# Query projection as two units of seven block products, w_down chunks moved around the last P7, idle TensorE instructions in two feed-forward jobs

## The chip, the core and the metric

The kernel runs on one core of a Trainium2 chip. A core has a matrix engine (TensorE, PE in the profile, with its weight loads as PEld), VectorE (DVE), ScalarE (ACT), GpSimd (POOL) and SyncE (SP). Each engine works off its own queue of instructions in a fixed order and waits for others by semaphores. DMAs are issued from SP's queue (plain copies) and, where the transfer adds to its destination, from POOL's. The metric is the device time of one execution in microseconds; lower is better.

## What is computed

One encoder layer on 512 tokens of width 1024, all in float32. After two mixers come memory cross-attention and a gated feed-forward layer; the change concerns these two.

```python
def memory_cross_attention(hn, memn, w_q, w_k, w_v, w_o):
    q = (hn @ w_q).reshape(bsz, seq, XATTN_HEADS, XATTN_HEAD_DIM)
    k = (memn @ w_k).reshape(bsz, MEM_LEN, XATTN_HEADS, XATTN_HEAD_DIM)
    v = (memn @ w_v).reshape(bsz, MEM_LEN, XATTN_HEADS, XATTN_HEAD_DIM)
    s = jnp.einsum('blhd,bmhd->bhlm', q, k) * (XATTN_HEAD_DIM ** -0.5)
    p = jax.nn.softmax(s, axis=-1)
    o = jnp.einsum('bhlm,bmhd->blhd', p, v).reshape(bsz, seq, D_MODEL)
    return o @ w_o

def swiglu(hn, w_gate, w_up, w_down):
    return (jax.nn.silu(hn @ w_gate) * (hn @ w_up)) @ w_down
...
    h = h + memory_cross_attention(rms_norm(h, xattn_norm_g[i]), memn, ...)
    h = h + swiglu(rms_norm(h, ffn_norm_g[i]), w_gate[i], w_up[i], w_down[i])
```

There are 4 heads of 256, 256 memory rows, and a feed-forward width of 2816.

## The kernel before

**Precision.** Every float32 operand is split into a high part (ACT, a cast to fp32r, L85) and a low part (DVE, the difference, L86). A matrix product is then three fp32r matmuls: high by high, high by low, low by high (`mm3`).

**Weights and their plan.** All weight blocks, each 128 x 1024 elements (512 KB), stand in one list, `plan`, in the order in which TensorE uses them. `next_w` takes the next entry. At that point it also issues what has come due for later entries: a plain load from SP up to three entries ahead (`LOADS`; three `raw` buffers), the split into high and low two entries ahead (`SPLITS`), and other transfers by the distance written beside them. `begin` runs these. The tile framework's scheduler, which goes by a simulated timeline, then decides the order of the instructions on each engine, except that instructions marked by `keep_in_program_order` (here `in_order`) keep their order among themselves.

**Block products.** The ten units of the feed-forward layer (512 columns each of w_gate and w_up, L1408 on) use Strassen's scheme in Winograd's form: the 2 x 2 blocks of tokens and weights are multiplied in seven block products P1 to P7 instead of eight, each 24 matmuls of 256 columns (`product`, L1306 on). Sums of weight blocks are made in part by adding DMAs of POOL onto tile `t` (`onto`, L177) and on DVE (L180); sums of activations on DVE. A job runs P5, P6, (P1 of the next unit), P7, (P2 of the next unit), P4, P3. P6, P7 and P4 add up in one PSUM bank `px`; after P6 and after P7 ACT copies the bank's state (`u2` L1421, `u3` L1428). In the last job two chunks of w_down's first product stand between P6 and P7, and nothing between P7 and P4. w_down is done in the same scheme over the tokens' 256-row halves; its weight sums are made by DMA alone, ahead of time, in DRAM scratch `dsum`: for each of 24 pieces a plain copy from SP (`start`, L236) and, three plan entries later, an adding DMA from POOL (`add`, L239), from entry 14 on every third entry.

**Queries.** hn is turned to feature-major form by TensorE transposes (`to_feat`, L485) and split. Each head is one `feat` over two blocks of w_q: 96 matmuls of 256 columns for the first head (two token parts) and 48 of 512 for each other head. Then come `scores` (24 matmuls of 256 columns, softmax on DVE and ACT), `turn_probs` (8 transposes) and `values` (12 matmuls of 512 columns), the values of a head after the scores of the next. w_k and w_v go before, in blocks of half length (256 memory rows); w_xo goes after.

Of the kernel before, what the change touches and what calls it, by code (L numbers as in the profile page):

```python
# [30 lines left out]
XH = 4  # L31
# [21 lines left out]
def hybrid_layer_kernel(  # L53
# [108 lines left out]
    def plan_unit(w, c0):  # L162

        kh = KD // 2
        b = lambda i, j: block(w, i * kh, kh, c0 + 256 * j, 256)
        r = {}

        def fresh(nm):
            r[nm] = (wp if nm == "b11" else stp[0]).tile([P, kh, 256], F32, tag="raw" if nm == "b11" else nm,
                                                         name=nm, bufs=3 if nm == "b11" else 2)  # L170
            return r[nm]

        def plain(nm, src):
            return lambda: nc.sync.dma_start(fresh(nm), src)

        def onto(nm, src):
            return lambda: nc.gpsimd.dma_start(r[nm], src, accum_op=ALU.add)  # L177

        def tt(o, x, y, op):
            nc.vector.tensor_tensor(r[o], r[x], r[y], op)  # L180
# [9 lines left out]
        return {q: ((w, c0, q), loads, made) for q, loads, made in (  # L190
            (1, [(4, plain("b11", b(0, 0)))], make("b11")),
            (2, [(4, plain("b21", b(1, 0)))], make("b21")),
            (5, [(7, plain("t", b(0, 0))), (5, onto("t", b(0, 1))), (5, plain("b22", b(1, 1)))],
             make("t", "t", "t", "b22", ALU.add)),
            (6, [], lambda: (make("t", "b11", "t", "b11", ALU.subtract)(), tt("t", "t", "b21", ALU.add))[0]),
            (7, [], make("b11")),
            (4, [], make("t")),
            (3, [], make("b22")))}

    def plan_units(units, down):  # L200


        made = [plan_unit(*u) for u in units]
# [25 lines left out]
    def plan_sums(first, step):  # L229


        more = {5: lambda c: down_block(0, 1, c), 7: lambda c: down_block(1, 1, c),
                6: lambda c: down_sum(5, c), 4: lambda c: down_sum(6, c)}

        def start(q, i, jc, c):
            tc.keep_in_program_order(nc.sync.dma_start(down_sum(q, c), down_block(i, jc, c)))  # L236

        def add(q, c):
            nc.gpsimd.dma_start(down_sum(q, c), more[q](c), accum_op=ALU.add)  # L239

        j = first
        for q, i, jc in ((5, 0, 0), (7, 0, 1), (6, 1, 1), (4, 1, 0)):
            for c in range(CHUNKS):
                plan[j][1].append((0, lambda x=(q, i, jc, c): start(*x)))
                plan[j + step][1].append((0, lambda x=(q, c): add(*x)))
                j += step
# [39 lines left out]
    for c0 in range(0, D, 256):  # L286
        plan_feat(w_q, c0, KD)
# [8 lines left out]
    plan_sums(first_copy + 2, 3)  # L296
# [71 lines left out]
    def tokm(w, c0, act, nk, evac, ntok=NT, last=2, kpt=2, hook=None, cut=None, t0=0):  # L368
# [6 lines left out]
        for wi in range(nw):  # L375
            hi, lo = next_w(w, wi * kpt, kpt, c0, 512)
            held.append((wi, hi, lo))
            if hook is not None and wi == nw - last:
                hook()
# [99 lines left out]
    def to_feat(src, hi, lo, tsl, full=None, part=(0, 1)):  # L479

        for q in part:
            ps = aux("ptr", (P, 4, P))
            for j in range(4):
                k = 4 * q + j
                nc.tensor.transpose(ps[:, j, :], src[:, k * P:(k + 1) * P], ident)  # L485
            split(hi[:, 4 * q:4 * q + 4, tsl], lo[:, 4 * q:4 * q + 4, tsl], ps)
            if full is not None:
                nc.scalar.copy(full[:, 4 * q:4 * q + 4, tsl], ps)
# [3 lines left out]
    def norm_feat(src, g, hi, lo, tsl, ss=None, full=None):  # L492
        xs = xsp[0].tile([P, D], F32, tag="xs", name="xs", bufs=2)
        rms_scale(src, g, xs, ss)
        later(0.6, lambda: to_feat(xs, hi, lo, tsl, full))
# [602 lines left out]
    hn_hi, hn_lo = token_slot("hn")  # L1098
    hn = (hn_hi, hn_lo)
# [16 lines left out]
    for t in range(NM):  # L1116
        later(0.2 + t, lambda t=t: mem_norm(t))

# [15 lines left out]
    def feat_norm(g, hi, lo, full=None):  # L1134
        return lambda t, ss: norm_feat(h[:, t, :], g, hi, lo, slice(t * P, (t + 1) * P), ss, full)

    mg = (mg_hi, mg_lo)
    for half in range(2):
        tokm(w_out, half * 512, mg, KD, add_evac(half, 0, feat_norm(g_x, hn_hi, hn_lo)))
# [3 lines left out]
    shift = ap_.tile([P, APART[0]], F32, name="shift")  # L1143
    nc.gpsimd.memset(shift, 0.0)
    kt_hi = ap_.tile([P, KD, M], F32R, name="kt_hi")
    kt_lo = ap_.tile([P, KD, M], F32R, name="kt_lo")
    vt_hi = ap_.tile([P, NM, D], F32R, name="vt_hi")
    vt_lo = ap_.tile([P, NM, D], F32R, name="vt_lo")
# [4 lines left out]
    def v_evac(half):  # L1153
        def f(t, ps):
            cs = slice(half * 512, half * 512 + 512)
            split(vt_hi[:, t, cs], vt_lo[:, t, cs], ps)
        return f

    for c0 in range(0, D, 256):
# [5 lines left out]
    ot_hi = slot("D", (P, KD, T), F32R, "ot_hi")  # L1165
    ot_lo = slot("E", (P, KD, T), F32R, "ot_lo")
    qs = {}

    def q_evac(m, j, ps):
        if j == 0:  # L1170
            qq = mq_tile("qq", 0).rearrange("p (h k t) -> p h k t", h=2, k=2)
            qs[m // 2] = (qq[:, 0], qq[:, 1])
        q_hi, q_lo = qs[m // 2]
        split(q_hi[:, j, :], q_lo[:, j, :], ps)

    def scores(hd):
        q_hi, q_lo = qs.pop(hd)
        scale = XD ** -0.5
        probs = []
        for i in range(2):  # L1180
# [7 lines left out]
            prob = ap_.tile([P, 2, M], F32, tag="prob", name="prob", bufs=2)  # L1188
            probs.append(prob)
# [3 lines left out]
            for tt in range(2):  # L1193
                nc.scalar.activation(prob[:, tt, :], ps[:, tt, :], AF.Exp, bias=nm[:, tt:tt + 1],
                                     scale=scale, accum_out=sm[:, tt:tt + 1])
            nc.vector.reciprocal(rs, sm)
            for tt in range(2):
                nc.vector.tensor_scalar(prob[:, tt, :], prob[:, tt, :], rs[:, tt:tt + 1], None, ALU.mult)
        return probs

    def turn_probs(hd, probs):
        p_hi = ap_.tile([P, NM, T], F32R, tag="p_hi", name="p_hi", bufs=2)
        p_lo = ap_.tile([P, NM, T], F32R, tag="p_lo", name="p_lo", bufs=2)
        for mt in range(NM):
            ps = aux("ppt", (P, NT, P))
            for t in range(NT):
                nc.tensor.transpose(ps[:, t, :], probs[t // 2][:, t % 2, mt * P:(mt + 1) * P], ident)
# [3 lines left out]
    def values(hd, p_hi, p_lo):  # L1211
        for dt_ in range(2):
            ps = bank("po")
            cs = slice(hd * XD + dt_ * P, hd * XD + dt_ * P + P)
            for mt in range(NM):
                mm3(ps, (vt_hi[:, mt, cs], vt_lo[:, mt, cs]), (p_hi[:, mt, :], p_lo[:, mt, :]), mt == 0, mt == NM - 1)
            split(ot_hi[:, 2 * hd + dt_, :], ot_lo[:, 2 * hd + dt_, :], ps)

    pts = []
# [13 lines left out]
    tokm(w_xo, 0, ot, KD, add_evac(0, 1, None), hook=lambda: values(XH - 1, *pts.pop()))  # L1233
# [49 lines left out]
    K0, K1, T0, T1 = slice(0, 4), slice(4, 8), slice(0, 256), slice(256, 512)  # L1283
# [22 lines left out]
    def product(ps, u, q, start):  # L1306

        hi, lo = next_w(u[0], u[1], q)
        for j in range(2):
            cs = slice(j * P, (j + 1) * P)  # L1310
            for k in range(4):
                a = (hi[:, k, cs], lo[:, k, cs])
                b = (ops[q][0][:, k, :], ops[q][1][:, k, :])
                for i, (x, y) in enumerate(((0, 0), (0, 1), (1, 0))):
                    nc.tensor.matmul(ps[:, j, :], a[x], b[y], start=start and j == k == i == 0,  # L1315
                                     stop=k == 3 and i == 2, skip_group_check=True)
        tick(2.7)

    def unit_bank(name):
        return bank(name).rearrange("p (j t) -> p j t", j=2)  # L1320

    def unit_start(u):
        x, v = unit_bank("px"), unit_bank("pv")
        product(x, u, 1, True)
# [10 lines left out]
    def unit_second(u, v):  # L1335
        product(v, u, 2, False)
# [70 lines left out]

    for i, u in enumerate(UNITS):  # L1408
# [3 lines left out]
        product(q, u, 5, True)  # L1412
# [5 lines left out]
        product(x, u, 6, False)  # L1418
# [12 lines left out]
        if not final:  # L1431
            unit_second(UNITS[i + 1], begun[1])
        V.tensor_tensor(u3, q, u3, ALU.subtract)
        put(u, 1, T1, u3)
        product(x, u, 4, False)
# [4 lines left out]
        product(q, u, 3, False)  # L1440
# [133 lines left out]
```

## Time and profile before

| | us |
|---|---|
| runs shown (3): median, lowest, highest | 913.34, 913.03, 913.4 |
| profiled execution, device time | 914.3 |
| its span from first to last instruction | 912.5 |
| busy in it: PE, DVE, ACT, POOL | 899.1, 607.5, 460.1, 93.6 |

The page of the profile gives each engine's busy time; the stretches show it part by part; the chain of waits follows what ended last back through the engines; the groups list instructions by source line, engine and tile with their mean duration; a timeline lists them one by one. A matmul's listed duration includes the length of the engine's pipeline, so that durations of matmuls overlap; what a matmul costs in a row of them is the distance of their starts. DMA rows give size and time from issue to landing.

### The profile page before, as it was taken

Reading aid. Unit: us, or ns where it says so; the run is one execution under the profiler, and the core shown is the slowest. Engines: PE = TensorE matmul, PEld = TensorE weight load, DVE = VectorE, ACT = ScalarE, POOL = GpSimd, SP = SyncE. Lnnn points to the kernel's source line nnn. Section 1 sums busy time; section 2 is a strip of 40 time slices with the busy share of each in tenths; the row PEclk is TensorE's granted clock in tenths of the full one; section 3 lists DMA queues with packets and bytes.
Section 4 is the critical chain, followed back from the end, with each engine's and each line's share of the span. In section 5 each row is a group of like instructions: output and inputs, shape, how many; then the busy total and the mean of one; then the engine's idle time right before and its main releaser. Section 6 shows DMA issues by size and latency. Waiting matters only on the chain.

```text
span 912.5 us, 14202 instructions
## 1 busy us (share of the span) xinstructions
PE 899.1 (99%) x5546; PEld 789.3 (86%) x5546; DVE 607.5 (67%) x1002; ACT 460.1 (50%) x674; POOL 93.6 (10%) x157
## 2 busy tenths in 40 slices
PE   9999999999999999999999999999999999999996
PEld 6788888888888887889898888899999999888875
DVE  5596662888753235758545444787778777889875
ACT  5542985244374334346434433655454554655663
POOL 1004220000025300002000001000000000000010
PEclk9999999999999999999999999999999999999998
DMA  7445273675546656776995317416455553246672
GB/s 242 137 125 145 71 180 120 183 201 136 141 135 157 146 173 184 237 227 194 258 279 136 82 64 236 110 43 158 125 146 148 124 155 101 70 138 198 196 231 101
DMA packets 105158, 142.25 MB, mean 156 GB/s; under 512 B 13170, under 2 KB 73090, under 8 KB 105091
## 3 DMA queue, kind: packets, MB, share of 16 engines
q1 hardware_dynamic: 90114, 119.88, 41.0%
q0 software_dynamic: 12384, 20.42, 13.2%
q10 hardware_dynamic: 2592, 1.05, 0.5%
q8 instruction: 43, 0.70, 0.3%
q14 instruction: 25, 0.20, 0.1%
HBM read 134.54 MB, written 29.85 MB: 180 GB/s over the span
## 4 chain that ended last, share of the span: by engine, by line
PE 90%; ACT 4%; DMA 2%; DVE 1%; issue 1%; POOL 0%; POOLq 0%; SPq 0%; DVEq 0%; ACTq 0%
PE pf L327 33%; PE pt L327 14%; PE px L1315 12%; PE dx L327 6%; PE pq L1315 6%; PE dq L327 3%; PE pv L1315 3%; PE dv L327 2%; PE pk L764 2%; DMA wraw<-in_w_up_dram 1%; PE ptr L485 1%; PE po L327 1%; PE psc L327 1%; ACT whi L85 1%; PE psv L1012 1%
## 5 line engine op out<-in xcount | busy, mean ns | idle before, releaser
L86 DVE TENSOR_TENSOR wlo<-wraw,whi 128x1024 fp32r<-128x1024 f32 (+1 forms) x133 | 157.7, 1186 | 131.7 <-ACT whi L85 130.1
L85 ACT CAST whi<-wraw 128x1024 fp32r<-128x1024 f32 (+1 forms) x133 | 135.9, 1022 | 180.0 <-PE pf L327 83.4
L327 PE MATMUL pf<-xn,whi 128*128 128x512 f32 x448 | 140.0, 392 | 0.0
L327 PEld LDWEIGHTS pf<-xn,whi 128*128 128x128 f32 x448 | 83.5, 188 | 17.1 <-issue 0.2
L327 PE MATMUL pf<-xn,wlo 128*128 128x512 f32 x224 | 87.5, 391 | 0.0
L1315 PE MATMUL px<-fn,whi 128*128 128x256 f32 x480 | 83.8, 277 | 1.5 <-ACT u L1428 1.5
L1315 PEld LDWEIGHTS px<-fn,whi 128*128 128x128 f32 x480 | 72.6, 188 | 1.8 <-ACT u L1428 1.7
L85 ACT CAST whi<-b 128x1024 fp32r<-128x1024 f32 x40 | 42.2, 1054 | 54.2 <-PE px L1315 26.6
L86 DVE TENSOR_TENSOR wlo<-b,whi 128x1024 fp32r<-128x1024 f32 x40 | 48.9, 1222 | 27.4 <-ACT whi L85 27.4
L1315 PE MATMUL px<-fn,wlo 128*128 128x256 f32 x240 | 66.3, 276 | 0.0
L1315 PE MATMUL pq<-s,whi 128*128 128x256 f32 x320 | 55.0, 276 | 0.0
L327 PE MATMUL dx<-whi,s 128*128 128x512 f32 x170 | 53.5, 391 | 0.4 <-DVE h L1499 0.4
L327 PEld LDWEIGHTS pf<-xn,wlo 128*128 128x128 f32 x224 | 42.1, 188 | 8.7
L1315 PEld LDWEIGHTS pq<-s,whi 128*128 128x128 f32 x320 | 48.2, 188 | 0.0
L86 DVE TENSOR_TENSOR wlo<-t,whi 128x1024 fp32r<-128x1024 f32 x30 | 36.7, 1224 | 16.9 <-ACT whi L85 16.9
L85 ACT CAST whi<-t 128x1024 fp32r<-128x1024 f32 x30 | 31.6, 1054 | 32.2 <-PE pv L1315 11.3
L1315 PEld LDWEIGHTS px<-fn,wlo 128*128 128x128 f32 x240 | 45.1, 188 | 0.0
L327 PE MATMUL pt<-whi,xn 128*128 128x512 f32 x128 | 44.5, 420 | 0.1
L1315 PE MATMUL pq<-s,wlo 128*128 128x256 f32 x160 | 44.2, 276 | 0.0
L327 PE MATMUL pf<-hn,whi 128*128 128x512 f32 (+1 forms) x160 | 41.8, 348 | 0.0
L327 PEld LDWEIGHTS dx<-whi,s 128*128 128x128 f32 x170 | 31.8, 188 | 7.5 <-ACT whi L85 0.8
L327 PE MATMUL dx<-wlo,s 128*128 128x512 f32 x85 | 33.0, 390 | 0.0
(385 smaller groups left out, 2170.6 us busy)
## 6 DMA issues: line engine op xcount, KB each, us to landing
wraw<-in_w_in_dram SPq DMA_DIRECT2D x36, 512.0 KB, 3.8
dsum<-in_w_down_dram SPq DMA_DIRECT2D x20, 512.0 KB, 6.6
wraw<-dsum SPq DMA_DIRECT2D x20, 512.0 KB, 4.1
b<-in_w_gate_dram SPq DMA_DIRECT2D x15, 512.0 KB, 3.7
b<-in_w_up_dram SPq DMA_DIRECT2D x15, 512.0 KB, 3.6
wraw<-in_w_down_dram SPq DMA_DIRECT2D x15, 512.0 KB, 3.6
dsum<-in_w_down_dram POOLq DMA_DIRECT2D x10, 512.0 KB, 7.0
dsum<-dsum POOLq DMA_DIRECT2D x10, 512.0 KB, 6.0
```

The source lines that it names most:

```text
L85: hi = nc.scalar.copy(dst_hi, src)
L86: lo = nc.vector.tensor_tensor(dst_lo, src, dst_hi.bitcast(F32), ALU.subtract)
L327: m = nc.tensor.matmul(ps, a[x], b[y], start=start and i == 0, stop=stop and i == 2, skip_group_check=free)
L485: nc.tensor.transpose(ps[:, j, :], src[:, k * P:(k + 1) * P], ident)
L764: nc.tensor.matmul(ps[32 * j:32 * j + 32, q, :], bd[i][:, g].rearrange("p d c -> p (d c)"), lc(es[i], g), start=(i == 0), stop=False, tile ...
L1012: nc.tensor.matmul(ps[:, t * P:(t + 1) * P], zt[:, t, h * P:(h + 1) * P], wst[:, h, :], start=True, stop=True)
L1315: nc.tensor.matmul(ps[:, j, :], a[x], b[y], start=start and j == k == i == 0, stop=k == 3 and i == 2, skip_group_check=True)
```

## The change

1. **w_q becomes two units** of 512 columns, each in seven block products with the two halves of the tokens. The operands 1, 2, 7 and 4 stand in `hn`, whose high and low part now get the offsets `APART`; 5, 6 and 3 in the slots D and E, before `ot` takes them. hn is also kept unsplit (`hfull`); four DVE sums on it and four splits make the operands 5, 7, 6 and 3, and two splits of 512 columns are left out in exchange (`skip`). The bank's states are copied by ACT (`seed`, `kept`) and subtracted by DVE (`minus`); queries reach the scores through `query_part`. w_v's result takes `hfull`'s place. The order of heads changes: scores 0 and 1 stand between products of the second unit, then values 0, scores 2 and 3; the rest goes between the blocks of w_xo.
2. **w_q's block sums** 4 to 7 for both units are made in DRAM scratch (`qsum`), like `dsum`: eight pairs of copy and adding DMA more.
3. **Places of all 32 sums** in the plan are given anew: from entry 5 every third (12), from 40 every second (8), from 79 every third (3), from 116 every fifth (9, with the addition four entries later). Before they were 24, from entry 14 every third. w_q has 14 entries now instead of 8; entry 109 + 7(i - 1) is P5 of job i.
4. **The last job**: one w_down chunk stays between P6 and P7, the other goes between P7 and P4.
5. **Idle instructions**: in jobs 1 and 2, ahead of P5, P6, P7 and P4, transposes of the identity ("t") or matmuls of 512 columns ("p") into an unused bank, marked in order.
6. Unit 1's plain loads keep the program's order.

```diff
-    def plan_unit(w, c0):
+    def plan_unit(w, c0, ordered=False):
...
-            return lambda: nc.sync.dma_start(fresh(nm), src)
+            def f():
+                ins = nc.sync.dma_start(fresh(nm), src)
+                if ordered:
+                    in_order(ins)
+            return f
...
+    QSRC = {1: (0, 0), 2: (1, 0), 3: (1, 1)}
+    qsum = {(q, n): dp.tile([P, KD // 2, 256], F32, name=f"qsum{q}{n}") for q in (4, 5, 6, 7) for n in range(2)}
...
+        for q, n in ((1, 0), (5, 0), (2, 0), (6, 0), (1, 1), (7, 0), (2, 1), (4, 0), (3, 0),
+                     (6, 1), (7, 1), (5, 1), (4, 1), (3, 1)):
...
+                nc.sync.dma_start(got["raw"], query_block(*QSRC[q], n) if q in QSRC else qsum[q, n])
...
-            between = [nx[1]] if nx else down[:2]
-            plan.extend([m[5], m[6]] + between + [m[7]] + ([nx[2]] if nx else []) + [m[4], m[3]])
+            between = [nx[1]] if nx else down[:1]
+            plan.extend([m[5], m[6]] + between + [m[7], nx[2] if nx else down[1], m[4], m[3]])
...
+        for (dst, src, more), (j, step) in zip(jobs, places):
+            plan[j][1].append((0, lambda d=dst, x=src: tc.keep_in_program_order(nc.sync.dma_start(d, x))))
+            plan[j + step][1].append((0, lambda d=dst, x=more: nc.gpsimd.dma_start(d, x, accum_op=ALU.add)))
...
-    plan_sums(first_copy + 2, 3)
+    plan_sums([(5 + 3 * i, 3) for i in range(12)] + [(40 + 2 * i, 2) for i in range(8)] +
+              [(79 + 3 * i, 3) for i in range(3)] + [(116 + 5 * i, 4) for i in range(9)])
...
-    hn_hi, hn_lo = token_slot("hn")
+    hn_hi, hn_lo = token_slot("hn", APART)
...
+    hfull = ap_.tile([P, KD, T], F32, tag="vt", name="hfull", bufs=1)
...
+    sd, se = (slot(tag, (P, KD * T), F32R, "hs" + tag.lower()) for tag in "DE")
+    part_at = lambda t, i: t[:, i:i + 1024].rearrange("p (k n) -> p k n", k=4)
+    hops[6], hops[5] = halves_at(sd, 4, 256, APART), halves_at(se, 4, 256, APART)
+    hops[3] = (part_at(sd, 2176 + APART[0]), part_at(se, 2048 + APART[1]))
+
+    def token_sums():
+        h11, h12, h21, h22 = (hfull[:, k, t] for t in (T0, T1) for k in (K0, K1))
+        for q, dst, x, y, op in ((5, h22, h21, h22, ALU.subtract), (7, h21, h11, h21, ALU.subtract),
+                                 (6, h11, h22, h11, ALU.subtract), (3, h12, h12, h11, ALU.add)):
+            nc.vector.tensor_tensor(dst, x, y, op)
+            later(0.5 * len(sums), lambda q=q, dst=dst: split(*hops[q], dst))
+            sums.append(q)
+
+    sums = []
+    later(2, token_sums)
...
-    for hd in range(XH):
-        feat(w_q, hd * XD, hn, KD, q_evac, parts=2 if hd == 0 else 1)
-        probs = scores(hd)
-        if hd > 0:
-            values(hd - 1, *pts.pop(0))
-        later(1, lambda hd=hd, probs=probs: pts.append(turn_probs(hd, probs)))
+    def seed(x):
+        v = unit_bank("qv")
+        nc.scalar.copy(v, x)
+        return v
+
+    def kept(x, name):
+        t = np_.tile([P, 2, 256], F32, tag="ev", name=name, bufs=2)
+        nc.scalar.copy(t, x)
+        return t
+
+    def minus(x, t):
+        nc.vector.tensor_tensor(t, x, t, ALU.subtract)
+        return t
...
+    qx, qq_ = unit_bank("qx"), None
+    query_product(qx, 0, 1, True)
+    qv = seed(qx)
+    qq_ = unit_bank("qq")
+    query_product(qq_, 0, 5, True)
+    query_product(qv, 0, 2)
+    query_part(0, T0, qv)
+    query_product(qx, 0, 6)
+    u2 = kept(qx, "u2")
...
+    query_product(x1, 1, 6)
+    u2 = kept(x1, "u2")
+    probs0 = scores(0)
+    query_part(2, T0, v1)
+    query_product(x1, 1, 7)
...
+    values(0, *pts.pop(0))
+    probs2 = scores(2)
+    probs3 = scores(3)
+    turn(1, probs1)
...
-    tokm(w_xo, 0, ot, KD, add_evac(0, 1, None), hook=lambda: values(XH - 1, *pts.pop()))
+    tokm(w_xo, 0, ot, KD, add_evac(0, 1, None), hooks={1: second, 2: last_two})
...
+    def between(*what):
+
+        rest_ = aux("idle")
+        for w in what:
+            if w == "t":
+                in_order(nc.tensor.transpose(rest_[:, 0:P], ident, ident))
+            else:
+                in_order(nc.tensor.matmul(rest_, ops[1][0][:, 0, 0:P], fn_hi[:, 0, :], start=True, stop=True))
+
     for i, u in enumerate(UNITS):
...
+        if i in (1, 2):
+            between(*"tt")
+        product(q, u, 5, True, ops)
...
+        if i in (1, 2):
+            between(*"pt"[:i])
+        product(x, u, 6, False, ops)
...
-            down_product(dx, 1, True, range(2))
-        product(x, u, 7, False)
+            down_product(dx, 1, True, range(1))
+        if i in (1, 2):
+            between(*"tttt"[:i * 2 - 1])
+        product(x, u, 7, False, ops)
...
+        else:
+            down_product(dx, 1, True, range(1, 2))
...
+        if i in (1, 2):
+            between(*("tttt", "tt")[i - 1])
+        product(x, u, 4, False, ops)
```

Written out, job 1 gets "tt", "p", "t", "tttt" and job 2 "tt", "pt", "ttt", "tt".

More of the change, by code (lines that the diff above doesn't have):

```diff
@@ L198, in plan_unit, with query_block, plan_queries, load @@
             (3, [], make("b22")))}
+    QSRC = {1: (0, 0), 2: (1, 0), 3: (1, 1)}
+    qsum = {(q, n): dp.tile([P, KD // 2, 256], F32, name=f"qsum{q}{n}") for q in (4, 5, 6, 7) for n in range(2)}
+    def query_block(i, j, n):
+        return block(w_q, i * KD // 2, KD // 2, 512 * n + 256 * j, 256)
+    def plan_queries():
+        for q, n in ((1, 0), (5, 0), (2, 0), (6, 0), (1, 1), (7, 0), (2, 1), (4, 0), (3, 0),
+                     (6, 1), (7, 1), (5, 1), (4, 1), (3, 1)):
+            got = {}
+            def load(q=q, n=n, got=got):
+                got["raw"] = wp.tile([P, KD // 2, 256], F32, tag="raw", name="wraw", bufs=3)
+                nc.sync.dma_start(got["raw"], query_block(*QSRC[q], n) if q in QSRC else qsum[q, n])
+            plan.append(((w_q, 512 * n, q), [(LOADS, load)], lambda got=got: halves(got.pop("raw"))))
     def plan_units(units, down):
-        made = [plan_unit(*u) for u in units]
+        made = [plan_unit(*u, ordered=i == 1) for i, u in enumerate(units)]
         for i in range(2):
@@ L227, in down_sum, with plan_sums @@
         return dsum[q][:, 2 * c:min(2 * c + 2, NF // 2), :]
[L229 to L242, printed above, removed]
-            for c in range(CHUNKS):
-                plan[j][1].append((0, lambda x=(q, i, jc, c): start(*x)))
-                plan[j + step][1].append((0, lambda x=(q, c): add(*x)))
-                j += step
+    def plan_sums(places):
+        jobs = []
+        for q, first, more in ((5, (0, 0), lambda n: query_block(0, 1, n)), (7, (0, 1), lambda n: query_block(1, 1, n)),
+                               (6, None, lambda n: query_block(1, 1, n)), (4, None, lambda n: query_block(1, 0, n))):
+            for n in range(2):
+                jobs.append((qsum[q, n], qsum[q + (-1 if q == 6 else 2), n] if first is None else query_block(*first, n),
+                             more(n)))
+        for q, i, jc, more in ((5, 0, 0, lambda c: down_block(0, 1, c)), (7, 0, 1, lambda c: down_block(1, 1, c)),
+                               (6, 1, 1, lambda c: down_sum(5, c)), (4, 1, 0, lambda c: down_sum(6, c))):
+            for c in range(CHUNKS):
+                jobs.append((down_sum(q, c), down_block(i, jc, c), more(c)))
+        assert len(jobs) == len(places)
+        for (dst, src, more), (j, step) in zip(jobs, places):
+            plan[j][1].append((0, lambda d=dst, x=src: tc.keep_in_program_order(nc.sync.dma_start(d, x))))
+            plan[j + step][1].append((0, lambda d=dst, x=more: nc.gpsimd.dma_start(d, x, accum_op=ALU.add)))
     def plan_down(w, make_tokens, entries):
@@ L285, in hybrid_layer_kernel @@
         plan_tok(w_v, half * 512, KD)
-    for c0 in range(0, D, 256):
-        plan_feat(w_q, c0, KD)
+    plan_queries()
     plan_tok(w_xo, 0, KD)
@@ L377, in tokm @@
             held.append((wi, hi, lo))
-            if hook is not None and wi == nw - last:
-                hook()
+            if wi in hooks:
+                hooks[wi]()
             if wi < nw - last:
@@ L477, in rms_scale, with to_feat @@
             nc.vector.scalar_tensor_tensor(dst[:, HALF[i]], src[:, HALF[i]], r, g[:, HALF[i]], ALU.mult, ALU.mult)
-    def to_feat(src, hi, lo, tsl, full=None, part=(0, 1)):
+    def to_feat(src, hi, lo, tsl, full=None, skip=None, part=(0, 1)):
         for q in part:
@@ L1117, in hybrid_layer_kernel @@
         later(0.2 + t, lambda t=t: mem_norm(t))
+    shift = ap_.tile([P, APART[0]], F32, name="shift")
+    nc.gpsimd.memset(shift, 0.0)
+    hfull = ap_.tile([P, KD, T], F32, tag="vt", name="hfull", bufs=1)
     g_x = gain(xattn_norm_g[0], "g_x")
@@ L1132, in add_evac, with feat_norm @@
         return f
-    def feat_norm(g, hi, lo, full=None):
-        return lambda t, ss: norm_feat(h[:, t, :], g, hi, lo, slice(t * P, (t + 1) * P), ss, full)
+    def feat_norm(g, hi, lo, full=None, skip=False):
+        return lambda t, ss: norm_feat(h[:, t, :], g, hi, lo, slice(t * P, (t + 1) * P), ss, full,
+                                       0 if skip and t >= 2 else None)
     mg = (mg_hi, mg_lo)
     for half in range(2):
-        tokm(w_out, half * 512, mg, KD, add_evac(half, 0, feat_norm(g_x, hn_hi, hn_lo)))
+        tokm(w_out, half * 512, mg, KD, add_evac(half, 0, feat_norm(g_x, hn_hi, hn_lo, hfull, True)))
     mn = (mn_hi, mn_lo)
-    shift = ap_.tile([P, APART[0]], F32, name="shift")
-    nc.gpsimd.memset(shift, 0.0)
     kt_hi = ap_.tile([P, KD, M], F32R, name="kt_hi")
     kt_lo = ap_.tile([P, KD, M], F32R, name="kt_lo")
-    vt_hi = ap_.tile([P, NM, D], F32R, name="vt_hi")
-    vt_lo = ap_.tile([P, NM, D], F32R, name="vt_lo")
+    vts = []
     def k_evac(m, j, ps):
@@ L1154, in f @@
         def f(t, ps):
+            if not vts:
+                vt = ap_.tile([P, 2, NM, D], F32R, tag="vt", name="vt", bufs=1)
+                vts.extend((vt[:, 0], vt[:, 1]))
+            vt_hi, vt_lo = vts
             cs = slice(half * 512, half * 512 + 512)
@@ L1215, in values, with product @@
             for mt in range(NM):
-                mm3(ps, (vt_hi[:, mt, cs], vt_lo[:, mt, cs]), (p_hi[:, mt, :], p_lo[:, mt, :]), mt == 0, mt == NM - 1)
+                mm3(ps, (vts[0][:, mt, cs], vts[1][:, mt, cs]), (p_hi[:, mt, :], p_lo[:, mt, :]), mt == 0, mt == NM - 1)
             split(ot_hi[:, 2 * hd + dt_, :], ot_lo[:, 2 * hd + dt_, :], ps)
-    pts = []
-    for hd in range(XH):
-        feat(w_q, hd * XD, hn, KD, q_evac, parts=2 if hd == 0 else 1)
-        probs = scores(hd)
-        if hd > 0:
-            values(hd - 1, *pts.pop(0))
-        later(1, lambda hd=hd, probs=probs: pts.append(turn_probs(hd, probs)))
+    def product(ps, u, q, start, ops):
+        hi, lo = next_w(u[0], u[1], q)
+        for j in range(2):
+            cs = slice(j * P, (j + 1) * P)
+            for k in range(4):
+                a = (hi[:, k, cs], lo[:, k, cs])
+                b = (ops[q][0][:, k, :], ops[q][1][:, k, :])
+                for i, (x, y) in enumerate(((0, 0), (0, 1), (1, 0))):
+                    nc.tensor.matmul(ps[:, j, :], a[x], b[y], start=start and j == k == i == 0,
+                                     stop=k == 3 and i == 2, skip_group_check=True)
+        tick(2.7)
@@ new lines, in unit_bank, with query_product @@
+    def unit_bank(name):
+        return bank(name).rearrange("p (j t) -> p j t", j=2)
+    def query_product(ps, n, q, start=False):
+        product(ps, (w_q, 512 * n), q, start, hops)
+    def seed(x):
[9 more added lines that the diff above has]
+        return t
@@ new lines, in hybrid_layer_kernel, with turn @@
+    pts = {}
+    def turn(hd, probs):
+        pts[hd] = turn_probs(hd, probs)
+    qx, qq_ = unit_bank("qx"), None
[7 more added lines that the diff above has]
+    u2 = kept(qx, "u2")
+    x1 = unit_bank("qx")
+    query_product(x1, 1, 1, True)
+    v1 = seed(x1)
+    query_product(qx, 0, 7)
+    u3 = kept(qx, "u3")
+    query_product(v1, 1, 2)
@@ new lines, in hybrid_layer_kernel @@
+    query_part(1, T1, minus(qq_, u3))
+    query_product(qx, 0, 4)
+    query_part(0, T1, qx)
+    query_product(qq_, 0, 3)
+    query_part(1, T0, minus(qq_, u2))
+    query_product(x1, 1, 6)
[3 more added lines that the diff above has]
+    query_product(x1, 1, 7)
+    u3 = kept(x1, "u3")
+    qq_ = unit_bank("qq")
+    query_product(qq_, 1, 5, True)
+    u3 = minus(qq_, u3)
+    query_product(x1, 1, 4)
+    query_part(2, T1, x1)
+    turn(0, probs0)
+    query_product(qq_, 1, 3)
@@ L1228, in hybrid_layer_kernel, with second, last_two @@
+    u2 = minus(qq_, u2)
+    probs1 = scores(1)
+    query_part(3, T1, u3)
+    query_part(3, T0, u2)
+    ot_hi = slot("D", (P, KD, T), F32R, "ot_hi")
+    ot_lo = slot("E", (P, KD, T), F32R, "ot_lo")
+    values(0, *pts.pop(0))
+    probs2 = scores(2)
+    probs3 = scores(3)
+    turn(1, probs1)
+    def second():
+        values(1, *pts.pop(1))
+        turn(2, probs2)
+        turn(3, probs3)
+    def last_two():
+        for i in (2, 3):
+            values(i, *pts.pop(i))
     g_f = gain(ffn_norm_g[0], "g_f")
@@ L1304, in hybrid_layer_kernel @@
     ops = {1: fn_q(K0, T0), 2: fn_q(K1, T0), 7: fn_q(K0, T1), 4: fn_q(K1, T1)}
[L1306 to L1320, printed above, removed]
     def unit_start(u):
         x, v = unit_bank("px"), unit_bank("pv")
-        product(x, u, 1, True)
+        product(x, u, 1, True, ops)
         nc.scalar.copy(v, x)
```

47 lines of the change are left out of this document (21 added, 26 removed).

## The prediction

> **What bounds the kernel now.** I read the page first, for the engine that is never free.
>
> ```profile
> span 912.5 us, 14202 instructions
> PE 899.1 (99%) x5546; PEld 789.3 (86%) x5546; DVE 607.5 (67%) x1002; ACT 460.1 (50%) x674; POOL 93.6 (10%) x157
> PEclk9999999999999999999999999999999999999998
> ```
>
> TensorE (PE) is busy for 99% of the span at full clock, VectorE (DVE) for 67%, ScalarE (ACT) for 50%. So time is won by fewer TensorE columns or by closing one of its few gaps, and lost by anything that makes it wait. Second, the busy times by stretch: w_k, w_v, the queries with scores and values, the feed-forward jobs but the last, and the last job.
>
> ```profile
> core 0: us, PE busy (x) PEld busy (x) DVE busy (x) ACT busy (x) POOL busy (x), PEclk, DMA share, GB/s
> 418.00:443.00 25.00, 25.00 (x217) 24.96 (x216) 21.00 (x31) 15.24 (x25) 3.60 (x4) 1.00 0.76 232
> 443.00:465.50 22.50, 22.50 (x99) 18.29 (x98) 11.39 (x12) 10.34 (x12) 1.61 (x2) 1.00 0.90 244
> 465.50:532.80 67.30, 67.15 (x398) 59.24 (x398) 34.94 (x63) 27.64 (x55) 3.26 (x4) 1.00 0.53 149
> 600.00:786.00 186.00, 186.00 (x1643) 186.00 (x1643) 145.96 (x145) 97.49 (x117) 10.30 (x8) 1.00 0.47 120
> 786.00:803.00 17.00, 15.50 (x109) 14.10 (x109) 14.15 (x14) 10.07 (x11) 0.00 (x0) 1.00 0.32 109
> ```
>
> TensorE never waits in 186 us of jobs, although these work by the seven-product scheme that the queries are to get, with DVE busy 146 of 186 us; only the last job has a hole (15.50 of 17.00); and in the w_k stretch DVE is already busy 21.0 of 25.0 us.
>
> A matmul's listed duration includes its pipeline, so costs are taken from how fast matmuls follow each other. The chain of waits in order of time gives that (start, length, what, number):
>
> ```profile
> 443.31 22.40 PE pt L327 x96
> 465.71 11.50 PE pf L327 x96
> 515.39 7.06 PE pf L327 x31
> 522.45 0.87 PE ppt L1207 x8
> 647.60 5.44 PE pq L1315 x48
> 814.47 14.96 PE dq L327 x66
> ```
>
> 256-column matmuls of the first query head: 11.50/96 = 0.120 us; 512-column ones of a later head: 7.06/31 = 0.228; a transpose: 0.87/8 = 0.109; a 256-column matmul of a product: 5.44/48 = 0.1133, so its 24 take 2.72; a 512-column matmul in the w_down products: 14.96/66 = 0.227. A w_v block of 512 KB lasts 22.40/8 = 2.80.
>
> **The change part by part.**
>
> **1. Queries.** The group of the tile hn counts what goes:
>
> ```profile
> L327 PE MATMUL pf<-hn,whi x160: 274/389/476, 465.5 to 526.6; 128*128 128x512 f32 x96, 128*128 128x256 f32 x64
> L327 PE MATMUL pf<-hn,wlo x80: 283/389/400, 466.0 to 526.8; 128*128 128x512 f32 x48, 128*128 128x256 f32 x32
> ```
>
> Removed: 96 at 256 columns (11.5 us) and 144 at 512 (144 x 0.228 = 32.8), together 44.3 us. Added: 14 products of 24 matmuls, 336 x 0.1133 = 38.1 us; I take the jobs' 0.1133 and not the first head's 0.120 because hn now gets the two offsets (APART) that the feed-forward operands have; at 0.120 it would be 40.3. Gain 6.2 us, at worst 4.0.
>
> The Trainium skill, page "TensorE: Matmul & The Clock Gate", section "Back-to-back issue gap", speaks against narrowing: in streams of weight load and matmul it has 81 ns per matmul at 128 columns and 131 ns at 512. An estimate on the line between them is 98 ns at 256, so 336 x 98 = 32.8 against 192 x 131 = 25.2 us for the same queries unsplit, a loss of 7.6. This trace differs: 227 and 113.3 ns in just such streams, half for half, and the measurement decides.
>
> **2. The last job.** The hole, from the timelines of PE and ACT:
>
> ```profile
> 797.20 0.28 PE L1315 MATMUL px<-fn,wlo 128*128 128x256 f32 x1
> 798.99 0.50 PE L1315 MATMUL px<-fn,whi 128*128 128x256 f32 x2 [1.50 <-ACT u L1428]
> 797.40 1.04 ACT L85 CAST whi<-wraw 128x1024 fp32r<-128x1024 f32 x1 [0.71 <-PE px L1315]
> 798.36 0.58 ACT L1428 COPY u<-px 128x512 f32<-128x512 f32 x1
> ```
>
> P4 adds onto the bank that P7 filled and must wait until ACT has copied it (L1428), behind a weight split in ACT's queue. From 797.20 to 798.99 are 1.79 us, less a matmul's 0.11: a hole of 1.67. The second w_down chunk now stands there: 12 matmuls, 12 x 0.227 = 2.72, which covers it. Next late could be P7, which waits for the like copy after P6; it still has the first chunk's 2.72 before it, where 1.67 is needed. Gain 1.7; nothing if the scheduler puts the chunk elsewhere.
>
> **3. Idle instructions.** "tt","p","t","tttt" and "tt","pt","ttt","tt" make 15 transposes and 2 products of 512 columns: 15 x 0.109 + 2 x 0.227 = 1.63 + 0.45 = 2.1 us. They stand where PE is busy 186.00 of 186.00, so nothing covers them: cost 2.1 in full, 0 only if PE comes to wait at those places anyway.
>
> **4. Query operands and PSUM copies on DVE and ACT.** The nearest rows:
>
> ```profile
> L86 DVE TENSOR_TENSOR wlo<-wraw,whi 128x1024 fp32r<-128x1024 f32 (+1 forms) x133 | 157.7, 1186 | 131.7 <-ACT whi L85 130.1 <-issue 0.8
> L85 ACT CAST whi<-wraw 128x1024 fp32r<-128x1024 f32 (+1 forms) x133 | 135.9, 1022 | 180.0 <-PE pf L327 83.4 <-PE pt L327 28.2 <-issue 17.4
> L180 DVE TENSOR_TENSOR t<-t,b 128x1024 f32<-128x1024 f32 x20 | 24.4, 1220 | 0.3
> L86 DVE TENSOR_TENSOR hn<-ptr,hn 128x512 fp32r<-128x512 f32 x8 | 5.4, 682 | 0.0
> L1433 DVE TENSOR_TENSOR u<-pq,u 128x512 f32<-128x512 f32 x10 | 6.8, 684 | 0.0
> L488 ACT COPY full<-ptr 128x512 f32<-128x512 f32 x8 | 4.7, 587 | 3.5 <-DVE fn L86 3.4
> ```
>
> Around w_k DVE gets four token sums (4 x 1.22) and four operand splits (4 x 1.19) and loses two hn splits (2 x 0.68): +8.3 us. Against 21.00 of 25.00 that is 4.3 too many for w_k alone, but over w_k and w_v it is 21.0 + 11.4 + 8.3 = 40.7 of 47.5, so it fits if it spreads. ACT gets eight full copies (8 x 0.59), four splits and loses two: +7.6 on 25.6 of 47.5, hidden. What is queued behind the sums on DVE are weight splits, for which PE waits; they run up to two blocks, 2 x 2.72, ahead. In the query stretch DVE gets six more weight splits and four subtractions: 34.9 + 7.1 + 2.7 = 44.8 of 61.1 us (67.3 - 6.2), ACT six splits and six copies: 27.6 + 6.1 + 3.5 = 37.2. Each PSUM copy has a product or a score block of 2.72 before its bank is written again; a cover gone would cost 1.67 each, as in the last job. Bounds: 0, for the jobs run so without a wait, and 4.3, DVE's excess in w_k. I take 0.8, a fifth of the upper end, as the jobs are the nearer row.
>
> The loads: 14 blocks of 512 KB, one per 2.72, as dense as w_v's one per 2.80, which cost PE nothing at a DMA share of 0.90. No sums are planned any more from entry 57 to 78, so the stretch before is emptier: cost 0, within the 4.3.
>
> **5. The places of the sums.** Eight query sums join the 24 of w_down; early ones keep a distance of three entries and begin three places (nine entries) earlier. What such a sum can cost (waits of POOL, the chain, PE's timeline):
>
> ```profile
> POOL dsum L239 <- DMA dsum<-in_w_down_dram: 210.7, 22, 18.3
> 121.70 4.36 DMA dsum<-in_w_down_dram
> 126.67 0.97 POOL dsum L239
> 127.73 1.35 POOL r L962
> 135.73 0.66 PE L814 MATMUL pw<-ident,wsx 128*128 128x128 f32 x4 [1.00 <-ACT zh L827]
> ```
>
> An adding DMA on POOL waits for its plain DMA; behind it stand the norm's r, then ACT, then PE, which idles 1.00. With three more pairs in this part and the phase kept, I take 0; bounds are -1.0 (that wait goes) and +3.0 (each new pair makes one). In w_out the pairs stand two entries apart (10.9 us at 0.227 a matmul), with the norms' r (L462) behind them: inside the same bounds. In the jobs the sums are new:
>
> ```profile
> 626.80 1.32 POOL L177 DMA_DIRECT2D t<-in_w_gate_dram  x1 [37.49 <-DVE a_up L1333]
> t<-in_w_gate_dram POOLq DMA_DIRECT2D x5, 512.0 KB, 6.0
> dsum<-in_w_down_dram SPq DMA_DIRECT2D x20, 512.0 KB, 6.6
> ```
>
> A plain DMA lands in 6.6 us, its addition comes four entries (four products, 10.9) later. The add to t of job 2 is issued at 626.80; job 2's P5 starts at 647.60 + 2.72 = 650.32 (the 48 matmuls of that piece are job 1's P3 and job 2's P5). Of these 23.5 us the add takes 6.0 and P5's split 2.2, so 15.3 are slack: cost 0. SP's share, one issue more per five entries, lies in the same slack; so do unit 1's ordered loads.
>
> **Sum.** -6.2 - 1.7 + 2.1 + 0.8 + 0 = -5.0 us. The profiled execution took 914.3 (1.8 beyond its span), so 909.3 for it; it stood 1.0 above the median 913.34, and the prediction in terms of the median is 908.3.
>
> **The rivals.**
>
> *A, the idles cost nothing*: PE waits at those places for splits that come later in the changed order. For: DVE is busy 78% there. Against: no wait in 186 us. Time 908.3 - 2.1 = 906.2.
>
> *B, DVE becomes the bound in w_k*: the sums stand in a block ahead of the weight splits and the 4.3 us come out as waits. For: 21.0 of 25.0 busy already. Against: two blocks of lead, and w_v has room. Time 908.3 - 0.8 + 4.3 = 911.8.
>
> *C, slower: POOL's queue in the jobs.* A sum's add waits ahead of t's add, so that P5 of the next job is late. For: POOL has waited 18.3 us for such a DMA. Against: with the planned distances no wait is due. It decides from a wait of 15.3 on; one of 18.3 makes P5 3.0 late, and with three of the nine places so the time is 908.3 + 9.0 = 917.3.
>
> *D, narrower matmuls don't pay*: every 256-column matmul keeps the first head's 0.120, and the chunk doesn't fill the hole: 908.3 + 2.2 + 1.7 = 912.2, no change by measure.
>
> The skill's line in part 1 is D's stronger form; by it the time would be 908.3 + 6.2 + 7.6 = 922.1, and with the trace against it I give that no chance of its own.
>
> **How the numbers follow.** Forecast 0.63, A 0.11, B 0.13, C 0.10, D 0.03. The forecast's own range is 906 to 910.5. The whole range goes down to A with the early wait gone (906.2 - 1.0 - 0.8 = 904.4) and up to B with a new early wait (911.8 + 1.0 = 912.8); C is left out, and with a few per cent below, that is under 2 in 10. What this kernel's measurement tells from no change is about 0.2%, 1.8 us: faster is below 911.5. The forecast is faster in 0.61 of its 0.63, A wholly, B in 0.05 of 0.13, the rest of these and D are the same, C is slower, as are 0.02 of B: faster 0.77, same 0.11, slower 0.12.
>
> **What would show it.** Right: 14 products in the query stretch, 2.72 each, the stretch about 6 us shorter; in the last job no gap over 0.5 us between P7 and P4, with w_down matmuls there; two of the jobs together longer by 2.1, PE still without a wait in them. Wrong: PE waiting for ACT's or DVE's weight splits in w_k or the queries (B), P5 waiting for t's DMA (C), PE idle just around the idle transposes (A). The forecast falls if the query products run at other than 0.113 us a matmul, or a PE wait of over 2 us stands anywhere from 60 to 800 us that wasn't there.

## The result, and the profile after

| | us |
|---|---|
| before, median of 5 runs | 913.04 (911.69 to 913.4) |
| changed, median of 5 runs | 909.59 (908.83 to 911.12) |
| ratio, 95% interval | 0.996 (0.9949 to 0.9972) |
| profiled executions, device time | 914.3 before, 908.83 after |

The change gains 3.45 us by the medians; 5.0 were forecast. The page of the changed kernel's profile:

```profile
span 907.0 us, 14526 instructions
PE 895.5 (99%) x5659; PEld 791.6 (87%) x5659; DVE 623.5 (69%) x1018; ACT 475.6 (52%) x696; POOL 104.3 (12%) x165
```

The spans differ by 5.5 us. The chain of waits in order of time (start, length, what, number) says where. First the kernel before, with the rows that the prediction did not show:

```profile
33.24 7.95 PE pt L327 x27
595.92 16.32 PE pf L327 x144
612.24 2.72 PE pq L1315 x24
780.88 5.44 PE pq L1315 x48
802.08 2.83 PE pq L1315 x24
804.91 9.56 PE dx L327 x42
```

The same places in the changed kernel, and all of its jobs 0 to 2:

```profile
33.24 6.35 PE pt L350 x27
...
464.14 2.74 PE qx L1276 x24
...
505.66 2.72 PE qq L1276 x24
...
588.18 16.96 PE pf L350 x144
605.14 2.83 PE pq L1276 x24
607.97 8.48 PE px L1276 x72
...
625.15 2.83 PE pq L1276 x24
628.21 5.45 PE px L1276 x48
633.77 2.76 PE px L1276 x24
636.53 2.72 PE pv L1276 x24
639.69 2.83 PE px L1276 x24
642.52 2.83 PE pq L1276 x24
645.56 2.74 PE pq L1276 x24
648.64 5.66 PE px L1276 x48
654.63 2.83 PE px L1276 x24
657.46 2.83 PE pv L1276 x24
660.51 2.74 PE px L1276 x24
663.25 5.44 PE pq L1276 x48
...
777.49 5.44 PE pq L1276 x48
...
799.71 8.61 PE dx L350 x38
```

What is to be seen first is a thing the prediction had not reckoned with. A product of 24 matmuls takes either 2.72 us, as in jobs 0 to 8 of the kernel before, or 2.83, as in the last product of its job 9 (802.08): **two paces**, 113.3 and 117.8 ns a matmul. Rows of 2.73 to 2.76 are fast products whose first matmul came a little late. In the changed kernel the stream of matmuls is slow from before 588 us (all seven products of job 0 are slow), turns fast at 628, slow at 639, fast at 645, slow at 648 and fast at 660, where it stays until the last job. Each of these turns stands where an idle group does, in the holes between the rows (627.98 to 628.21, 639.25 to 639.69 and so on). Some groups turn nothing (those ahead of 625.15, 633.77 and 654.63).

Differences of the starts, after less before:

| stretch | before | after | difference |
|---|---|---|---|
| to the first query product (465.71, 464.14) | 465.71 | 464.14 | -1.57 |
| queries, scores, values, w_xo, gate, to P5 of job 0 (612.24, 605.14) | 146.53 | 141.00 | -5.53 |
| P5 of job 0 to P5 of job 9 (780.88 + 2.72, 777.49 + 2.72) | 171.36 | 175.07 | +3.71 |
| last job up to w_down (804.91, 799.71) | 21.31 | 19.50 | -1.81 |
| the rest (912.5, 907.0) | 107.59 | 107.29 | -0.30 |

The first difference comes from the piece at 33.24 us (7.95 against 6.35 us for 27 matmuls). The changed kernel issues its first copy of a query sum at 37.16 us, inside this piece, so its place alone does not clear the change. Two runs below do: the kernel before with only the w_down chunk moved takes 6.35 us here, and the changed kernel without its idles 7.94. So the difference belongs to the execution and not to the change. Without it the traces differ by 3.9, near the medians' 3.45.

Busy times of the changed kernel by stretch (us, then busy PE, PEld, DVE, ACT and POOL, the granted clock, the DMA share and GB/s): w_k, the products up to w_xo, a slow job, a fast one and the last job.

```profile
416.60:441.70 25.10, 25.10 (x218) 25.09 (x217) 23.35 (x32) 20.51 (x33) 1.85 (x2) 1.00 0.49 157
464.10:517.20 53.10, 53.10 (x458) 52.55 (x457) 37.25 (x62) 32.17 (x59) 2.48 (x3) 1.00 0.74 219
605.00:624.00 19.00, 19.00 (x164) 19.00 (x163) 14.23 (x16) 9.97 (x12) 2.20 (x2) 1.00 0.70 190
665.00:684.00 19.00, 19.00 (x170) 19.00 (x169) 13.63 (x15) 9.64 (x12) 3.91 (x4) 1.00 0.86 205
783.00:800.00 17.00, 17.00 (x122) 15.77 (x121) 13.91 (x14) 10.43 (x12) 0.00 (x0) 1.00 0.36 109
```

PE counts as busy 19.00 of 19.00 us in the slow and in the fast job, at a granted clock of 1.00 in both; only the number of matmuls differs, 164 against 170. So the busy share hides the slow pace, the clock is not its cause, and the fuller DMA isn't either: 0.70 in the slow job, 0.86 in the fast one. In the last job the hole is gone (17.00 of 17.00), and w_k keeps PE busy throughout although DVE rose to 23.35 of 25.10.

### The profile page after: what moved, and what is told of

Same layout as the page of the kernel before. It is cut to its first block, busy times and chain, and to the rows that moved or that the text cites. A ratio compares the mean times of both kernels' runs of the same rounds, so it can differ in the third digit from the quotient of the medians.

```text
span 907.0 us, 14526 instructions
## 1 busy us (share of the span) xinstructions
PE 895.5 (99%) x5659; PEld 791.6 (87%) x5659; DVE 623.5 (69%) x1018; ACT 475.6 (52%) x696; POOL 104.3 (12%) x165
## 4 chain that ended last, share of the span: by engine, by line
PE 92%; ACT 3%; DMA 2%; issue 1%; DVE 1%; POOL 0%; SPq 0%; POOLq 0%; DVEq 0%; ACTq 0%
PE pf L350 28%; PE pt L350 16%; PE px L1276 12%; PE dx L350 6%; PE pq L1276 6%; PE dq L350 3%; PE pv L1276 3%; PE qx L1276 2%; PE dv L350 2%; PE pk L789 2%; PE ptr L509 1%; PE psc L350 1%; PE qq L1276 1%; PE po L350 1%; DMA xt<-in_x_dram 1%
## 5 line engine op out<-in xcount | busy, mean ns | idle before, releaser
L86 DVE TENSOR_TENSOR wlo<-wraw,whi 128x1024 fp32r<-128x1024 f32 (+1 forms) x139 | 165.1, 1188 | 109.2 <-ACT whi L85 107.6
L85 ACT CAST whi<-wraw 128x1024 fp32r<-128x1024 f32 (+1 forms) x139 | 142.5, 1025 | 163.1 <-PE pf L350 70.5
L1276 PEld LDWEIGHTS pq<-s,wlo 128*128 128x128 f32 x160 | 30.1, 188 | 0.0
```

Source lines behind the costliest of these rows:

```text
L85: hi = nc.scalar.copy(dst_hi, src)
L86: lo = nc.vector.tensor_tensor(dst_lo, src, dst_hi.bitcast(F32), ALU.subtract)
```

## The experiments

**The changed kernel again.** No edit. Is the pace fixed for a program?

> The changed kernel once more, unaltered. In its first trace the matmuls of the block products follow each other at 113.3 ns in most places, but at 117.8 ns from 575 to 628 us and again from 639 to 660 us, and the pace only changes where a transpose or another foreign instruction stands in the stream. Theory T (two paces, chosen anew at each disturbance by something that is fixed for a given program): the same stretches are slow again, time within 1 us of 909.6. Rival R (the pace is drawn anew in each execution): other stretches are slow, the time differs by 0.11 us for each product that changes its pace.

Measured: 908.53 (ratio 0.9958, 0.9946 to 0.9971). Its products are slow and fast at the same places, turning at 627.6, 639.1, 645.0, 648.1 and 659.9 us. In these two executions the pace belongs to the program and not to the execution, so rival R falls.

**Without the idles.**

```diff
-        if i in (1, 2):
-            between(*"tt")
...
-        if i in (1, 2):
-            between(*"pt"[:i])
...
-        if i in (1, 2):
-            between(*"tttt"[:i * 2 - 1])
...
-        if i in (1, 2):
-            between(*("tttt", "tt")[i - 1])
```

> The changed kernel without any idle instruction. Prediction's own account (idles only cost): 2.1 us faster than the changed kernel, 907.5. Theory T (idles break the stream and so move it from the pace of 117.8 to that of 113.3 ns): the stream that is slow from 575 us on meets nothing that changes it up to the last job, so some 61 products stay 0.11 us slower instead of 13: +5.3 for those 48, -2.9 for the idles and the slow first matmul behind them, together 2.4 slower, about 912.

Measured: 912.26 (ratio to the kernel before 0.9996, 0.9988 to 1.0005), 3.7 slower than the changed kernel in the same set (908.53). Its chain shows the reason at any place of the jobs:

```profile
663.08 5.65 PE pq L1276 x48
668.73 8.48 PE px L1276 x72
```

Every product takes 2.83, from the first job to the last. So here the idles more than pay for themselves by the pace, and the account by which they only cost is wrong in sign. Without them the change as a whole gains nothing that can be measured.

**The idles alone, in the kernel before.** The function `between` and its four calls are added there, nothing else.

> The kernel before with nothing but the idle instructions. Prediction's account: +2.1, 915.1, every product as before at 2.72 us. Theory T: the stream before is at the fast pace from 595 us on and the idles can only keep it or move it to the slow one: +2.9 with the slow first matmul behind each group, up to +5.5 more if it ends up slow after the last group: 915.9 to 921.4.

Measured: 920.38 (ratio 1.0087, 1.0073 to 1.01), 8.05 slower. The chain through its jobs 1 and 2:

```profile
629.37 2.73 PE pq L1315 x24
...
640.87 2.83 PE px L1315 x24
...
661.80 2.76 PE px L1315 x24
...
667.51 2.83 PE px L1315 x24
670.34 5.65 PE pq L1315 x48
```

A stream that was fast throughout turns slow at 640.87, and then fast and slow once more. The last group, the same "tt" behind which the changed kernel is fast, turns it slow at 667.51, and it stays slow. The same instructions at the same places bring 3.7 in one kernel and cost 8.05 in the other.

**The w_down chunk alone, in the kernel before.**

```diff
-            between = [nx[1]] if nx else down[:2]
-            plan.extend([m[5], m[6]] + between + [m[7]] + ([nx[2]] if nx else []) + [m[4], m[3]])
+            between = [nx[1]] if nx else down[:1]
+            plan.extend([m[5], m[6]] + between + [m[7], nx[2] if nx else down[1], m[4], m[3]])
...
-            down_product(dx, 1, True, range(2))
+            down_product(dx, 1, True, range(1))
...
+        else:
+            down_product(dx, 1, True, range(1, 2))
```

> The kernel before with nothing but the w_down chunk moved between the last P7 and P4. Prediction: the hole of 1.67 us closes, 911.4, no other stage moves. Rival: the chunk's weights or tokens come later than the hole and a wait of about the same length opens before it: 913.0, unchanged.

Measured: 911.04 against 912.33, 1.3 less, but the interval of the ratio, 0.9974 to 1.0008, includes no change. What the time leaves open the chain shows: P7, the chunk and P4 follow each other without a hole.

```profile
790.15 2.83 PE px L1315 x24
792.98 2.76 PE dx L327 x12
795.74 2.83 PE px L1315 x24
```

P5 of job 9 starts at 781.84 here and w_down at 801.39, which is 19.55 us against 21.31 in the kernel before.

**One group at one place.** If any foreign instruction (one that is not a matmul of the products) can turn the pace, one group early in the jobs could do better than eight. In the kernel without idles, ahead of P5 of job 0, for "t", "tt", "p" and "tttt":

```diff
         q = unit_bank("pq")
+        if i == 0:
+            between(*"t")
         product(q, u, 5, True, ops)
```

> The changed kernel with all idles of jobs 1 and 2 taken out and one single transpose ahead of P5 of job 0. Theory T (any foreign instruction makes the stream choose its pace anew, and it keeps the choice until the next): either the stream is fast from about 606 us to the last job, then some 68 products are 0.11 us shorter, 7.4 less than the kernel without idles (912.3), about 905; or it stays slow, 912.5. Rival U (what counts is the number of matmuls or the buffers in use at the places of jobs 1 and 2, not the disturbance): slow, 912.5, for this and the three others of this set.

> As the kernel with one transpose ahead of P5 of job 0, but with two. Theory T: 905 or 912.5, with no way to tell which; of the four kernels of this set about two should be fast. Rival U: 912.5.

> As before with one matmul of 512 columns in place of the transposes, ahead of P5 of job 0. Theory T: 905 or 912.5. A closer theory T2, that the matmul of 512 columns, which in both kernels with idles was followed by the fast pace, brings the fast pace: 905. Rival U: 912.5.

> As before with four transposes ahead of P5 of job 0. Theory T: 905.5 or 913. Rival U: 913. A closer theory T3, that an even number of foreign instructions keeps the pace and an odd one changes it: slow here and with two transposes, fast with one transpose and with one matmul.

| ahead of P5 of job 0 | median, us | ratio to before | products behind it |
|---|---|---|---|
| one transpose | 906.12 | 0.9905 (0.9872 to 0.9938) | 2.72 |
| two | 912.75 | 0.9983 (0.9965 to 1.0) | 2.83 |
| one 512-column matmul | 908.03 | 0.9918 (0.9888 to 0.9948) | 2.72 |
| four | 913.33 | 0.9984 (0.9962 to 1.0007) | 2.83 |

The chain with one transpose, then with two:

```profile
605.05 0.11 PE idle L1527
605.16 2.74 PE pq L1276 x24
```

```profile
603.88 0.22 PE idle L1527 x2
604.10 2.83 PE pq L1276 x24
```

One transpose of 0.11 us brings the kernel to 906.12, where two leave it at 912.75 in the same set, and none left it at 912.26 in another. The kernels with one and with two differ in a single transpose, and all their other matmuls stand in the same order in both traces, so rival U falls. By the ratio, 0.9905 with an interval that ends (0.9938) below the changed kernel's (0.9949 on), this version beats the changed kernel as well as the kernel before. T2 is not refuted: a 512-column matmul standing alone was followed by the fast pace here, at 628.21 in the changed kernel, and in the kernel before with the idles (job 1).

**Is it odd and even?** Odd numbers had turned the stream, even ones not. Three more kernels on the same base: "ttt" ahead of P5 of job 0, "t" ahead of P5 of jobs 0 and 1, "t" ahead of P5 of job 1 alone.

> The kernel without the idles of jobs 1 and 2, three transposes ahead of P5 of job 0. Theory T3 (an odd number of foreign instructions changes the pace of the stream, an even one keeps it; so it was with 1, 2, 4 transposes and one matmul at this place): fast, 113.3 ns, about 906.4. Theory T (the new pace has no such rule): slow, 912.7, as likely.

> One transpose ahead of P5 of job 0 and one ahead of P5 of job 1. T3: fast in job 0, slow from job 1 on, about 912. T: fast from job 1 on as well is as likely, 906.3. In the changed kernel a single transpose in a fast stream left it fast, against T3.

> One transpose ahead of P5 of job 1 alone. T3: slow up to there, fast behind, about 0.8 more than with the transpose in job 0, 906.9. T: as likely slow throughout, 912.4.

Measured, against a kernel before at 913.55: three transposes 912.54 (0.9974, 0.9946 to 1.0002), slow; in jobs 0 and 1 906.31 (0.9904, 0.9866 to 0.9942), fast behind both; in job 1 alone 906.91 (0.9908, 0.9875 to 0.994), slow up to 626.57 us and fast from there, as T3 had it too. The chain with both:

```profile
606.73 0.11 PE idle L1527
606.84 2.74 PE pq L1276 x24
...
625.90 0.11 PE idle L1527
626.01 2.76 PE pq L1276 x24
```

T3 falls twice: three transposes leave the stream slow, and the second single one leaves it fast. In these kernels a lone transpose always led to the fast pace, from slow and from fast; but in the kernel before with the idles, the "t" ahead of P7 of job 1 turned a fast stream slow (640.87). No rule of number covers all of it. Nor does the place in TensorE's queue: from P5 of job 1 on, this kernel with "t" twice and the one with "tt" have equally many transposes ahead and the same matmuls in the same order, and one is fast there and the other slow.

**The same elsewhere?** In the fastest version, one more transpose ahead of w_v.

```diff
+    in_order(nc.tensor.transpose(aux("idle")[:, 0:P], ident, ident))
     for half in range(2):
         tokm(w_v, half * 512, mn, KD, v_evac(half), ntok=NM)
```

> The fastest so far (one transpose ahead of P5 of job 0) with one more transpose ahead of w_v, whose 512-column matmuls run at 233.3 ns in all traces, against 226.7 elsewhere. If w_v's pace is of the same kind: 96 x 6.6 ns = 0.6 less, 905.5, and the first half at 226.7. If it comes from where w_v's operands lie: 233.3 as before, 906.2.

Without it w_v takes 22.40 us as in the kernel before; the chain with it:

```profile
441.57 0.11 PE idle L1212
441.68 21.99 PE pt L350 x96
```

w_v's 96 matmuls take 21.99 instead of 22.40 us, 229 instead of 233 ns on average. That is part of the way to 226.7, and neither of the two outcomes that were expected, but it shows that the pace of 512-column matmuls can be moved too. The whole is 906.12 (0.9896, 0.9861 to 0.9932), the same median as without it in another set; 0.3 us net can't be told by the time.

## Why the prediction came out as it did

**Direction and range.** Faster with 0.77, and 909.59 lies between 904.4 and 912.8. By the medians the gain was 3.45 where 5.0 stood, so the sum is 1.5 us off. That the time lies in the range is in part luck. Behind the last idle group the stream happened to be fast; had that group left it slow, as it did in the kernel before, the 46 products from there to P6 of job 9 would have taken 0.108 us more each. By this estimate that is 5.0 us, and 914.6 lies outside the range.

**Queries, -6.2: right.** The 14 products run at 2.72 each (464.14 on; 464.10 to 517.20 without a wait), so 38.1 us as worked out. The pace of the jobs came as forecast and the first head's 0.120 did not, but that hn's offsets (APART) bring it was not tested; the jobs, with such offsets, ran at both paces.

**The last job, -1.7: right**, measured -1.81. The first chunk alone covers P7's wait, as argued, and the stretch of the last job is without a wait.

**Idle instructions, +2.1: right as a cost, wrong as an account, and this is the step that failed.** The prediction had them stand where "nothing covers them: cost 2.1 in full", and the jobs' own products unchanged at 2.72. Jobs 0 to 8 became 3.71 longer. Fourteen of their products are slow, 14 x 0.11 = 1.5; the other 2.2 are the idles themselves. The step took the pace of 0.1133 for a property of the instruction. It belongs to the stream, and the changed kernel comes to its jobs with a slow one (588.18: 144 matmuls in 16.96 us, 117.8 ns; before 16.32, 113.3). That is +0.6 there and +1.5 in the jobs, together 2.1, more than the whole shortfall of 1.5; the waits below, less than their term, make up the rest. Had the idles not stood there, the time would have been 3.7 longer, as the run without them shows. Rival A had the idles' cost at nothing, for a wait that they would fill; there is no such wait. Their worth is another.

**Waits of the new order, +0.8: about nothing.** B fell: w_k shows no wait at DVE 23.35 of 25.10. What came is in w_xo, where values and blocks alternate (PE's timeline):

```profile
526.21 0.50 PE L350 MATMUL pt<-whi,ot_hi 128*128 128x512 f32 x1 [0.26 <-ACT ot_hi L85]
535.90 0.50 PE L350 MATMUL pt<-whi,ot_hi 128*128 128x512 f32 x1 [0.68 <-ACT ot_hi L85]
```

These 0.9 us of waiting for a value's split (0.26 + 0.68) are of the size that was put down. Yet the stretch as a whole came out at -5.53: -6.2 for the queries and +0.6 for the slow gate products leave +0.1 for all waits, gone and new.

**The sums' places, 0: right.** The early wait stayed (the chain has a query sum's DMA there now), and C did not come, although POOL waited up to 52.4 us for a sum (the chain, POOL's waits, and its timeline with the add to t of job 2):

```profile
120.07 4.42 DMA qsum<-in_w_q_dram
POOL dsum L268 <- DMA dsum<-in_w_down_dram: 229.4, 22, 52.4
620.18 1.33 POOL L181 DMA_DIRECT2D t<-in_w_gate_dram  x1 [2.31 <-DVE a_up L1447]
```

The add for job 2 went out at 620.18, its P5 began at 645.56: 25.4 us of lead against 23.5 before. D fell too.

The estimate that the prediction drew from the Trainium skill's two figures ("TensorE: Matmul & The Clock Gate", "Back-to-back issue gap"), by which the narrower matmuls lose, does not hold here at either pace: 336 x 0.1178 = 39.6 us are still less than 44.3.

**What stays open.** What makes a stream settle at one pace or the other was not found. The runs show that it repeats between two executions of the same program, that it holds through hundreds of matmuls and over changes of operands and banks, that transposes and lone matmuls can turn it, and that neither their number nor their place decides alone. Operand addresses were not varied alone. The kernel before, too, enters its jobs fast for a reason that no run here isolates.

## What to carry to other kernels

Where one engine is busy throughout, read the distance of its instructions' starts stretch by stretch and not its busy share: 4% of TensorE's time hid here behind "19.00 of 19.00". One small instruction can move all of the stream behind it by 7 us and show in no busy share, so a step is judged on its own stretch first, and the pace behind it separately. Where a long uniform stream is found at the slow pace, a single transpose at its head is worth a trial, and has to be tried anew after each edit.

## What the runs showed of the hardware that had not been expected

The same matmuls, with the same operands and a granted clock of 1.00, run at 113.3 or 117.8 ns at 256 columns, by what went before them. At 512 columns w_v's ran at 233.3 ns, or at 229 on average behind a transpose; those of the w_down products run at 226.7. A transpose costs its own 0.11 us, and the choice that it makes lasted in the fastest version up to P6 of job 9, 65 products of 24 matmuls: 1,560 x 4.5 ns = 7.0 us for one transpose.
